# Two of four sums of weight quarters made by an adding DMA, and the second output block with its sign turned, in the gate and up products of a streaming encoder

## The chip, the cores and the metric

The kernel runs on one core of one Trainium2 chip. The metric is the device time of one execution of the whole kernel in microseconds (us); lower is better.

## The reference

One step of a two-layer encoder with 512 prompt rows and 64 sample rows of width 1024 (T = 576 rows in all), in float32. A layer has three parallel mixers, a cross-attention over 256 memory rows, and a gated feed-forward block. The change is in the last of these:

```
h = rmsnorm(x, g_ffn_norm)
x = x + (silu(h @ w_gate) * (h @ w_up)) @ w_down
```

`w_gate` and `w_up` are 1024 x 2816, `w_down` is 2816 x 1024.

## The kernel before

**Products.** Every float32 matmul is done in three: each operand is split into a high half H (rounded, made by ScalarE's copy, `copyA`) and a low half L (the rest, made by VectorE as source minus H; `split_to`, L467). `mm3` (L443) then adds H.H, H.L and L.H in PSUM. A weight tile is the stationary operand, 128 x 128; the activations, transposed, stream by with half of the 576 rows, HF = 288 columns.

**The feed-forward block.** The 2816 hidden columns are 11 pairs p of 256. Pair 0 (`first`) is computed plainly while the normalised activations of the second half become ready. For pairs 1 to 10, `gated` (L1696) computes two 1024 x 256 by 1024 x 576 products, gate and then up, each by a scheme of seven products instead of eight: the weight block and the activation block are each cut into 2 x 2 quarters, a11 (first 512 input rows, first 128 output columns), a12 (last 512 rows, first 128 columns), a21 (first 512 rows, last 128 columns), a22, and seven products of sums of quarters are combined. `wino_w` (L600) loads the 256 weight columns into a 1 MB tile (`wraw`, two buffers), makes the sums, and splits everything. `winograd` (L635) runs the products in the order 1, 2, 6, 5, 7, 4, 3, each 12 matmuls of 288 columns. It keeps intermediate results in PSUM or, through ScalarE, in tiles named `part`. VectorE adds the parts into gate and up tiles; `WNorm.sums` (L571) makes the matching sums of activation quarters once per layer.

**The weight side of the seven products, before.** Products 1, 2 and 4 use a11, a12 and a22. The other four use sums made by VectorE into two tiles named `sum`: s1 = a21 + a22 (product 5), s2 = s1 - a11 (product 6), z1 = a11 - a21 (product 7), z2 = a12 - s2 (product 3). Each tile of two sums is split together into tiles `sH` and `sL` (two buffers each): products 6 and 5 share one, products 7 and 3 the other. The plain quarters are split into `wH` and `wL` (three buffers each), which the down products use as well.

**Order of the work.** A pass of gate or up takes seven products; between up of one pair and gate of the next, half of the down product (`down`, L1751) of an earlier group of pairs runs. Each engine executes its own list of instructions, in an order that is fixed when the program is built from dependencies, buffer counts and estimated durations; the text's order gives priority, so weight splits for the next pass stand among the evacuations of the present one. A new load waits until the last reader of the buffer's old content is done. SyncE's queue issues the weight loads. GpSimd's queue is used at the kernel's start alone.

Of the kernel before, what the change touches and what calls it, by code (L numbers as in the profile page):

```python
# [10 lines left out]
F32 = mybir.dt.float32  # L11
F32R = mybir.dt.float32r
U32 = mybir.dt.uint32
AF = mybir.ActivationFunctionType
# [11 lines left out]
HF = T // 2  # L26
KD = D // 128
# [203 lines left out]
def tile_hybrid(ctx, tc, ins, outs):  # L231
    clock = tc.clock = Clock()
    nc = Engines(tc)
# [9 lines left out]

    uid = [0]
    phase = ["in"]
    UB = {"u": 3, "j": 4, "kp": 3, "sg": 3, "R": 1, "oS": 2, "gate": 3}
    WB = {"wH": 3, "wL": 3}
    PB = {"D": 3, "S": 2, "T": 3}

    def nm(s):  # L250
        uid[0] += 1
        return f"{phase[0]}.{s}_{uid[0]}"
# [8 lines left out]
    turn = {"pool": None, "close": None}  # L261
# [47 lines left out]
    def copyA(out, in_, scale=None):  # L309
        if scale is None:  # L310
            act(out, in_, AF.Copy)
        else:
            act(out, in_, AF.Identity, scale=scale)

    def tt(out, a, b, op, eng=None):
        (eng or nc.vector).tensor_tensor(out, a, b, op=op)

    def stt(out, a, s, b, op0, op1):
        nc.vector.scalar_tensor_tensor(out, a, s, b, op0=op0, op1=op1)
# [3 lines left out]
    def fetch_w(src, kt, n, src2=None):  # L323
        n1 = n
        if src2 is not None:
            n += src2.shape[1]
        raw = clock.tile(wp.tile([128, 2048], F32, tag="wraw", name=nm("wraw"), bufs=2), "wraw", 2)
        raw = raw[:, :kt * n].rearrange("p (k n) -> p k n", n=n)
        nc.sync.dma_start(raw[:, :, 0:n1], src.rearrange("(k p) n -> p k n", p=128))
        if src2 is not None:  # L330
            nc.sync.dma_start(raw[:, :, n1:n], src2.rearrange("(k p) n -> p k n", p=128))
        return raw
# [134 lines left out]
    def split_to(src, H, L):  # L467
        copyA(H, src)
        tt(L, src, H, SUB)

    def rstd_bcast(acc, ones, r, scale=1.0):
        n = acc.shape[1]
        w = HF if n > 512 else n
        for c in range(0, n, w):
            d = ps_("T")[:, 0:w]
            mm(d, ones, acc[:, c:c + w])
            act(r[:, c:c + w], d, AF.Ln, scale=scale, bias=eps1)
        act(r, r, AF.Exp, scale=-0.5)
# [49 lines left out]
    class WNorm:  # L528
# [42 lines left out]
        def sums(self):  # L571

            n = 4 * HF
            b11, b21, b12, b22 = (self.x[i][:, q * n:(q + 1) * n] for i in range(2) for q in range(2))
            t = big(name="tA")
            x, y = t[:, 0:n], t[:, n:2 * n]
            Ha, La, Hb, Lb = (big(F32R, "bT") for _ in range(4))
            tt(x, b12, b11, SUB)
            tt(y, b22, x, SUB)
            split_to(y, Ha[:, n:2 * n], La[:, n:2 * n])  # L580
            split_to(x, Ha[:, 0:n], La[:, 0:n])
            tt(x, b22, b12, SUB)
            split_to(x, Hb[:, 0:n], Lb[:, 0:n])
            tt(y, b21, y, SUB)
            split_to(y, Hb[:, n:2 * n], Lb[:, n:2 * n])
            self.p.update({5: (Ha, La, 0), 6: (Ha, La, 1), 7: (Hb, Lb, 0), 4: (Hb, Lb, 1)})

# [11 lines left out]

    def wino_w(src):  # L600

        raw = fetch_w(src, KD, 256)
        a11, a12, a21, a22 = (raw[:, q * 4:q * 4 + 4, m * 128:(m + 1) * 128] for m in range(2) for q in range(2))

        def split(x, own):
            H, L = (clock.tile((turn["pool"] if own else wp).tile([128, 1024], F32R, tag=tag, name=nm(tag),
                                                                  bufs=2 if own else WB[tag]), tag, 2 if own else WB[tag])
                    for tag in (("sH", "sL") if own else ("wH", "wL")))
            n = x.shape[1] * 128
            H, L = (y[:, 0:n].rearrange("p (k n) -> p k n", n=128) for y in (H, L))  # L610
            split_to(x, H, L)
            return H, L

        def sums():
            return clock.tile(turn["pool"].tile([128, 1024], F32, tag="sum", name=nm("sum"), bufs=2), "sum",
                              2).rearrange("p (k n) -> p k n", n=128)

        out = {}
        A = split(raw[:, :, 0:128], False)
        out[1], out[2] = (A, 0), (A, 4)  # L620
        s = sums()
        s2, s1 = s[:, 0:4, :], s[:, 4:8, :]
        tt(s1, a21, a22, ADD)
        tt(s2, s1, a11, SUB)
        B = split(s, True)
        out[6], out[5] = (B, 0), (B, 4)
        z = sums()
        tt(z[:, 0:4, :], a11, a21, SUB)
        tt(z[:, 4:8, :], a12, s2, SUB)
        C = split(z, True)  # L630
        out[7], out[3] = (C, 0), (C, 4)
        out[4] = (split(a22, False), 0)
        return out

    def winograd(w, xf, put):  # L635


        def product(d, p, more=False):

            (H, L), k0 = w[p]  # L640
            for k in range(4):
                mm3(d, H[:, k0 + k, :], L[:, k0 + k, :], xf.part(p, 0, k), xf.part(p, 1, k), not more and k == 0, k == 3, more)

        def keep(d):
            c = clock.tile(turn["pool"].tile([128, HF], F32, tag="part", name=nm("part"), bufs=4), "part", 4)
            copyA(c, d)
            return c

        x = ps_("D")[:, 0:HF]
        product(x, 1)  # L650
        c1 = keep(x)
        d = ps_("T")[:, 0:HF]
        product(d, 2)
        put(0, 0, d, c1)
        yield
        product(x, 6, True)
        c2 = keep(x)
        y = ps_("S")[:, 0:HF]
        product(y, 5)
        product(x, 7, True)  # L660
        c3 = keep(x)
        put(1, 1, y, c3)
        d = ps_("T")[:, 0:HF]
        product(d, 4)
        put(1, 0, d, c3)
        product(y, 3, True)
        put(0, 1, y, c2)
# [268 lines left out]
    def layer(l, xn):  # L936
# [759 lines left out]
        def gated(p, aH, aL, k0):  # L1696

            cs = lambda a: slice(a * HF, (a + 1) * HF)
            done, done2 = [0, 0], [0, 0]
            s = [u("gate") for _ in range(2)]  # L1700

            def gate(m, a, d, c):
                tt(s[m][:, cs(a)], d, c, ADD)
                done[m] += 1
                if done[m] == 2:
                    act(s[m], s[m], AF.Silu)

            run(winograd(wino_w(I["w_gate"][l, :, p * 256:(p + 1) * 256]), xf, gate))
            t = [u() for _ in range(2)]

            def up_(m, a, d, c):
                tt(t[m][:, cs(a)], d, c, ADD)
                done2[m] += 1
                if done2[m] == 2:
                    tt(t[m], t[m], s[m], MUL)
                    split_to(t[m], aH[:, k0 + m, :], aL[:, k0 + m, :])

            run(winograd(wino_w(I["w_up"][l, :, p * 256:(p + 1) * 256]), xf, up_))

# [117 lines left out]
```

## Time and profile before

| what | value |
|---|---|
| median of 3 runs | 1663.23 us (1661.26 to 1664.08) |
| the profiled execution | 1666.25 us |
| its span | 1664.5 us |
| TensorE (PE) busy | 1638.2 us (98%) |
| TensorE weight load (PEld) busy | 1532.3 us (92%) |
| VectorE (DVE) busy | 1216.0 us (73%) |
| ScalarE (ACT) busy | 897.1 us (54%) |
| GpSimd (POOL) busy | 142.2 us (9%) |
| DMA, share of 16 engines on SyncE's queue | 25.0% |
| granted TensorE clock | 0.994 |

The span is the time from the first to the last instruction that the profiler saw; the execution is a little longer. Busy time of TensorE counts overlapping pipelined matmuls once. Every operation that goes through the kernel's recording helper has the line L209, so rows are told apart by their tiles: `ffn0.sum` is a tile named `sum` of layer 0's feed-forward block.

### The profile page before, as it was taken

What the parts mean: (1) busy time and instruction counts of PE and PEld (TensorE: products, weight loads), DVE (VectorE), ACT (ScalarE), POOL (GpSimd) and SP (SyncE); (2) the same over time, 40 slices, a digit from 0 to 9 for tenths busy, and PEclk for the clock granted to TensorE, in tenths of its full rate; (3) what the DMA queues carried; (4) which work ended last, traced back from release to release, by engine and by line L of the source; (5) the groups of instructions that cost most, each with busy time, mean ns of one, the idle gap of its engine ahead of it and who ended that gap; (6) DMA issues with size and microseconds to landing.
All of it is one profiled execution on the core that took longest, in us unless ns stands there. A gap on an engine that the chain in (4) does not pass through costs nothing.

```text
span 1664.5 us, 30858 instructions
## 1 busy us (share of the span) xinstructions
PE 1638.2 (98%) x12279; PEld 1532.3 (92%) x12279; DVE 1216.0 (73%) x2508; ACT 897.1 (54%) x1915; POOL 142.2 (9%) x257
## 2 busy tenths in 40 slices
PE   8999999999999999999999999999999999999998
PEld 7989788699999999999998889877999999999998
DVE  5747798876798767666667488987678877667663
ACT  6436778665754443344443457886667453344431
POOL 3112351000000000000010133300000000000000
PEclk9999999999999999999999999999999999999999
DMA  5322230022123232322223313201211232332321
GB/s 168 118 69 65 75 111 26 27 77 77 52 77 102 77 102 77 102 93 85 81 75 97 93 40 118 67 27 39 89 52 56 97 102 77 102 99 79 101 77 58
DMA packets 113647, 133.30 MB, mean 80 GB/s; under 512 B 10610, under 2 KB 95712, under 8 KB 113504
## 3 DMA queue, kind: packets, MB, share of 16 engines
q1 hardware_dynamic: 113120, 131.30, 25.0%
q8 instruction: 97, 1.59, 0.4%
q14 instruction: 46, 0.38, 0.1%
q0 software_dynamic: 352, 0.03, 0.0%
q10 hardware_dynamic: 32, 0.01, 0.0%
HBM read 123.64 MB, written 7.68 MB: 79 GB/s over the span
## 4 chain that ended last, share of the span: by engine, by line
PE 81%; DVE 7%; issue 4%; ACT 3%; DMA 2%; POOL 1%; ACTq 0%; POOLq 0%; DVEq 0%
PE ffn0.D L209 10%; PE ffn1.D L209 9%; PE ffn0.T L209 7%; PE ffn0.S L209 7%; PE ffn1.T L209 6%; PE ffn1.S L209 6%; PE win1.D L209 6%; PE win0.D L209 4%; PE wout1.D L209 3%; PE wout0.D L209 3%; PE cross1.D L209 2%; PE cross0.D L209 2%; PE cross0.T L209 1%; PE cross1.T L209 1%; PE mlap0.T L209 1%
## 5 line engine op out<-in xcount | busy, mean ns | idle before, releaser
L209 ACT ACTIVATE ffn1.wH<-ffn1.wraw 128x1024 fp32r<-128x1024 f32 x64 | 59.4, 927 | 116.9 <-PE ffn1.T L209 61.7
L209 ACT ACTIVATE ffn0.wH<-ffn0.wraw 128x1024 fp32r<-128x1024 f32 x64 | 59.3, 927 | 111.5 <-PE ffn0.T L209 60.4
L209 DVE TENSOR_TENSOR ffn1.sL<-ffn1.sum,ffn1.sH 128x1024 fp32r<-128x1024 f32 x40 | 48.9, 1222 | 40.0 <-ACT ffn1.sH L209 39.9
L209 DVE TENSOR_TENSOR ffn0.sL<-ffn0.sum,ffn0.sH 128x1024 fp32r<-128x1024 f32 x40 | 48.9, 1222 | 39.6 <-ACT ffn0.sH L209 39.5
L209 DVE TENSOR_TENSOR ffn1.wL<-ffn1.wraw,ffn1.wH 128x1024 fp32r<-128x1024 f32 x64 | 67.6, 1056 | 8.3 <-ACT ffn1.wH L209 7.6
L209 DVE TENSOR_TENSOR ffn0.wL<-ffn0.wraw,ffn0.wH 128x1024 fp32r<-128x1024 f32 x64 | 67.5, 1055 | 8.3 <-ACT ffn0.wH L209 7.6
L209 PE MATMUL ffn0.D<-ffn0.bT,ffn0.sH 128*128 128x288 f32 x320 | 65.3, 296 | 0.1
L209 PE MATMUL ffn1.D<-ffn1.bT,ffn1.sH 128*128 128x288 f32 x320 | 65.1, 295 | 0.1
L209 ACT ACTIVATE ffn1.sH<-ffn1.sum 128x1024 fp32r<-128x1024 f32 x40 | 42.2, 1055 | 21.4 <-PE ffn1.S L209 21.2
L209 ACT ACTIVATE ffn0.sH<-ffn0.sum 128x1024 fp32r<-128x1024 f32 x40 | 42.2, 1055 | 21.1 <-PE ffn0.S L209 21.0
L209 POOL TENSOR_TENSOR win1.s<-win1.vg,rS 128x32 f32<-128x32 f32 (+1 forms) x5 | 2.9, 590 | 581.3 <-DVE win1.vg L209 580.2
L209 PEld LDWEIGHTS ffn0.D<-ffn0.bT,ffn0.sH 128*128 128x128 f32 x320 | 51.6, 189 | 1.0 <-ACT ffn0.part L209 0.6
L209 PEld LDWEIGHTS ffn1.D<-ffn1.bT,ffn1.sH 128*128 128x128 f32 x320 | 51.6, 189 | 0.7 <-ACT ffn1.part L209 0.6
L209 PE MATMUL ffn1.D<-ffn1.bT,ffn1.sL 128*128 128x288 f32 x160 | 47.5, 297 | 0.0
L209 PE MATMUL ffn0.D<-ffn0.bT,ffn0.sL 128*128 128x288 f32 x160 | 47.5, 297 | 0.0
L209 PE MATMUL win1.D<-win1.wH,ffn0.hH 128*128 128x256 f32 (+1 forms) x160 | 47.2, 295 | 0.0
L209 PE MATMUL win0.D<-win0.wH,in.hH 128*128 128x256 f32 (+1 forms) x160 | 47.1, 295 | 0.0
L209 PE MATMUL win0.D<-win0.wL,in.hH 128*128 128x256 f32 (+1 forms) x160 | 46.1, 288 | 0.3 <-DVE win0.wL L209 0.3
L209 PE MATMUL win1.D<-win1.wL,ffn0.hH 128*128 128x256 f32 (+1 forms) x160 | 46.1, 288 | 0.3 <-DVE win1.wL L209 0.3
L209 PE MATMUL win0.D<-win0.wH,in.hL 128*128 128x256 f32 (+1 forms) x160 | 45.9, 287 | 0.0
L209 PE MATMUL win1.D<-win1.wH,ffn0.hL 128*128 128x256 f32 (+1 forms) x160 | 45.9, 287 | 0.0
L209 ACT ACTIVATE ffn0.part<-ffn0.D 128x288 f32<-128x288 f32 x60 | 24.5, 409 | 38.4 <-PE ffn0.D L209 38.4
(972 smaller groups left out, 6522.2 us busy)
## 6 DMA issues: line engine op xcount, KB each, us to landing
ffn0.wraw<-in_w_gate_dram SPq DMA_DIRECT2D x11, 1024.0 KB, 5.3
ffn0.wraw<-in_w_up_dram SPq DMA_DIRECT2D x11, 1024.0 KB, 5.3
ffn0.wraw<-in_w_down_dram SPq DMA_DIRECT2D x11, 1024.0 KB, 5.1
ffn1.wraw<-in_w_gate_dram SPq DMA_DIRECT2D x11, 1024.0 KB, 5.3
ffn1.wraw<-in_w_up_dram SPq DMA_DIRECT2D x11, 1024.0 KB, 5.4
ffn1.wraw<-in_w_down_dram SPq DMA_DIRECT2D x11, 1024.0 KB, 5.0
win1.wraw<-in_w_in_dram SPq DMA_DIRECT2D x7, 1024.0 KB, 5.4
win0.wraw<-in_w_in_dram SPq DMA_DIRECT2D x6, 1024.0 KB, 5.7
```

Source lines behind the costliest of these rows:

```text
L209: r = fn(*args, **kw)
```

## The change

The second output block of gate and up (the last 128 columns of each pair) is computed with its sign turned. With a21 and a22 replaced by their negatives, all sums become plain additions: s1 = a21 + a22 (product 5), s3 = a11 + a21 (product 7), s2 = s1 + a11 (product 6), s4 = s2 + a12 (product 3), up to signs that move to the activation sums and to the output: `WNorm.sums` forms its sums with other signs and splits one of them with `split_neg`, the Silu of the second block gets a scale of -1, and the split of the second block's product is done by `split_neg`.

s1 and s3 are no longer made by VectorE. SyncE's queue loads a11 into the raw tile, a12 and a22 into the raw tile, a22 a second time into a new tile `sumD` (s1's place) and a11 a second time (s3's place). Then GpSimd's queue loads a21 twice, adding to s1 and to s3. VectorE adds s2 and s4 into a tile `sum`. Products 6 and 3 now share one split (F), products 5 and 7 the other (E). `sumD` has two buffers, `sum` one instead of two, the gate tiles two instead of three, `part` three instead of four.

```diff
-    UB = {"u": 3, "j": 4, "kp": 3, "sg": 3, "R": 1, "oS": 2, "gate": 3}
+    UB = {"u": 3, "j": 4, "kp": 3, "sg": 3, "R": 1, "oS": 2, "gate": 2}
...
+    def split_neg(src, H, L):
+        copyA(H, src, scale=-1.0)
+        stt(L, src, -1.0, H, MUL, SUB)
...
-            tt(x, b12, b11, SUB)
-            tt(y, b22, x, SUB)
-            split_to(y, Ha[:, n:2 * n], La[:, n:2 * n])
+            tt(x, b11, b12, SUB)
+            tt(y, b22, x, ADD)
+            split_neg(y, Ha[:, n:2 * n], La[:, n:2 * n])
...
-            tt(y, b21, y, SUB)
+            tt(y, y, b21, SUB)
...
-        raw = fetch_w(src, KD, 256)
-        a11, a12, a21, a22 = (raw[:, q * 4:q * 4 + 4, m * 128:(m + 1) * 128] for m in range(2) for q in range(2))
+        raw = clock.tile(wp.tile([128, 2048], F32, tag="wraw", name=nm("wraw"), bufs=2), "wraw", 2).rearrange("p (k n) -> p k n", n=256)
+        e, f = (clock.tile(turn["pool"].tile([128, 1024], F32, tag=tag, name=nm(tag), bufs=n), tag, n)
+                .rearrange("p (k n) -> p k n", n=128) for tag, n in (("sumD", 2), ("sum", 1)))
+        rows = src.rearrange("(k p) n -> p k n", p=128)
+        a11, a12, a21, a22 = ((slice(q * 4, q * 4 + 4), slice(m * 128, (m + 1) * 128)) for m in range(2) for q in range(2))
+        nc.sync.dma_start(raw[:, 0:4, 0:128], rows[:, a11[0], a11[1]])
+        nc.sync.dma_start(raw[:, 4:8, :], rows[:, 4:8, :])
+        s1, s3, s2, s4 = e[:, 0:4, :], e[:, 4:8, :], f[:, 0:4, :], f[:, 4:8, :]
+        for x, y in ((s1, a22), (s3, a11)):
+            nc.sync.dma_start(x, rows[:, y[0], y[1]])
+        for x in (s1, s3):
+            nc.pool_queue.dma_start(x, rows[:, a21[0], a21[1]], accum_op=ADD)
...
-        s = sums()
-        s2, s1 = s[:, 0:4, :], s[:, 4:8, :]
-        tt(s1, a21, a22, ADD)
-        tt(s2, s1, a11, SUB)
-        B = split(s, True)
-        out[6], out[5] = (B, 0), (B, 4)
-        z = sums()
-        tt(z[:, 0:4, :], a11, a21, SUB)
-        tt(z[:, 4:8, :], a12, s2, SUB)
-        C = split(z, True)
-        out[7], out[3] = (C, 0), (C, 4)
-        out[4] = (split(a22, False), 0)
+        tt(s2, s1, raw[:, 0:4, 0:128], ADD)
+        tt(s4, s2, raw[:, 4:8, 0:128], ADD)
+        F = split(f, True)
+        out[6], out[3] = (F, 0), (F, 4)
+        E = split(e, True)
+        out[5], out[7] = (E, 0), (E, 4)
+        out[4] = (split(raw[:, 4:8, 128:256], False), 0)
...
-            c = clock.tile(turn["pool"].tile([128, HF], F32, tag="part", name=nm("part"), bufs=4), "part", 4)
+            c = clock.tile(turn["pool"].tile([128, HF], F32, tag="part", name=nm("part"), bufs=3), "part", 3)
...
-                    act(s[m], s[m], AF.Silu)
+                    act(s[m], s[m], AF.Silu, scale=-1.0 if m else 1.0)
...
-                    split_to(t[m], aH[:, k0 + m, :], aL[:, k0 + m, :])
+                    (split_neg if m else split_to)(t[m], aH[:, k0 + m, :], aL[:, k0 + m, :])
```

## Rows read from the trace of the kernel before

**Rows 1.** The page: busy us (share of the span) and instructions of each engine.
```profile
PE 1638.2 (98%) x12279; PEld 1532.3 (92%) x12279; DVE 1216.0 (73%) x2508; ACT 897.1 (54%) x1915; POOL 142.2 (9%) x257
```
**Rows 2.** Stretches: from:to, length, busy us and instructions, clock, DMA share, GB/s.
```profile
435.00:440.00 5.00, 5.00 (x40) 5.00 (x39) 5.00 (x11) 3.67 (x7) 0.00 (x0) 1.00 0.59 198
...
455.00:460.00 5.00, 5.00 (x40) 5.00 (x40) 4.85 (x5) 3.81 (x5) 0.00 (x0) 1.00 0.00 0
...
440.00:476.00 36.00, 34.29 (x250) 33.28 (x249) 32.72 (x43) 24.66 (x40) 0.00 (x0) 1.00 0.09 30
476.00:836.80 360.80, 360.68 (x2715) 359.80 (x2714) 260.63 (x404) 155.64 (x213) 0.00 (x0) 1.00 0.29 91
```
**Rows 3.** TensorE in order of time: start, us, instruction, [idle before, releaser].
```profile
445.65 0.40 PE L209 MATMUL ffn0.D<-cross0.bH,ffn0.wH 128*128 128x288 f32 x1 [0.65 <-ACT cross0.bH L209]
...
447.04 0.40 PE L209 MATMUL ffn0.D<-cross0.bL,ffn0.wH 128*128 128x288 f32 x1 [0.73 <-DVE cross0.bL L209]
```
**Rows 4.** Chain of waits, layer 0's feed-forward block: start, us, what.
```profile
504.85 1.59 PE ffn0.D L209 x12
...
579.64 1.86 PE ffn0.D L209 x12
...
611.72 1.59 PE ffn0.D L209 x12
...
614.91 1.76 PE ffn0.D L209 x12
616.67 1.59 PE ffn0.S L209 x12
...
638.93 1.59 PE ffn0.D L209 x12
```
**Rows 5.** The tile `ffn0.sum`: duration ns min/median/max, first and last start.
```profile
L209 DVE TENSOR_TENSOR ffn0.sum<-ffn0.wraw x40: 680/687/695, 434.4 to 769.3; 128x512 f32<-128x512 f32 x40
```
**Rows 6.** VectorE in order of time, columns as in rows 3.
```profile
437.64 0.69 DVE L209 TENSOR_TENSOR ffn0.sum<-ffn0.wraw,ffn0.sum 128x512 f32<-128x512 f32 x1
...
443.04 2.63 DVE L209 TENSOR_TENSOR cross0.xs<-cross0.xs,cross0.u 128x1152 f32<-128x1152 f32 x2
...
610.58 0.69 DVE L209 TENSOR_TENSOR ffn0.sum<-ffn0.wraw 128x512 f32<-128x512 f32 x1 [1.04 <-DMA ffn0.wraw<-in_w_gate_dram]
...
613.29 0.45 DVE L209 TENSOR_TENSOR ffn0.gate<-ffn0.S,ffn0.part 128x288 f32<-128x288 f32 x1
613.66 1.22 DVE L209 TENSOR_TENSOR ffn0.sL<-ffn0.sum,ffn0.sH 128x1024 fp32r<-128x1024 f32 x1
```
**Rows 7.** ScalarE in order of time, the same passage.
```profile
612.27 1.04 ACT L209 ACTIVATE ffn0.sH<-ffn0.sum 128x1024 fp32r<-128x1024 f32 x1
...
614.37 0.39 ACT L209 ACTIVATE ffn0.part<-ffn0.D 128x288 f32<-128x288 f32 x1
```
**Rows 8.** DMA issues: out<-in, queue, count, KB each, us to landing.
```profile
ffn0.wraw<-in_w_gate_dram SPq DMA_DIRECT2D x11, 1024.0 KB, 5.3
...
win0.pl<-in_cache_mla_latent_dram SPq DMA_DIRECT2D x1, 256.0 KB, 3.9
...
in.grow<-in_g_cqn_dram POOLq DMA_DIRECT2D x1, 1.0 KB, 4.8
...
in.grow<-in_g_qn_dram POOLq DMA_DIRECT2D x1, 0.5 KB, 6.3
```
**Rows 9.** SyncE's queue in order of time: start, us, issue.
```profile
428.91 0.37 SPq L209 DMA_DIRECT2D ffn0.wraw<-in_w_gate_dram  x1
...
480.58 0.37 SPq L209 DMA_DIRECT2D ffn0.wraw<-in_w_gate_dram  x1
...
605.12 0.37 SPq L209 DMA_DIRECT2D ffn0.wraw<-in_w_gate_dram  x1
```
**Rows 10.** GpSimd in order of time, an issue of a small load.
```profile
2.76 0.49 POOL L209 DMA_DIRECT2D in.grow<-in_g_mem_norm_dram  x1
```
**Rows 11.** Groups by line and form: busy us, mean ns; the two forms of subtraction.
```profile
L209 DVE TENSOR_TENSOR ffn0.actL<-ffn0.u,ffn0.actH 128x576 fp32r<-128x576 f32 x22 | 16.6, 752 | 0.1
...
L209 DVE SCALAR_TENSOR_TENSOR ffn0.hL<-X,gT,ffn0.hH 128x576 fp32r<-128x576 f32 x8 | 6.5, 816 | 0.9 <-ACT ffn0.hH L209 0.8
```

More of the change, by code (lines that the diff above doesn't have):

```diff
@@ L612, in split @@
             return H, L
-        def sums():
-            return clock.tile(turn["pool"].tile([128, 1024], F32, tag="sum", name=nm("sum"), bufs=2), "sum",
-                              2).rearrange("p (k n) -> p k n", n=128)
         out = {}
```

## The prediction
> **What bounds the kernel now.** I read the busy times first, then stretches of the run, then what TensorE waited for, then the two transfers and engines that the change touches. TensorE is busy 1638.2 of 1664.5 us [rows 1]. The stretch table says where the rest is [rows 2]: from 476.0 to 836.8 us, where the first layer's feed-forward block runs on the seven-product scheme, TensorE is busy 360.68 of 360.80 us, VectorE 260.63 and ScalarE 155.64. The reader should see that VectorE has 100 us to spare there. All 20 gate and up passes of a layer lie in this stretch, bar the first 3 us, and layer 1 repeats it. A product of 12 matmuls takes 1.59 us, one after another, in the chain of waits [rows 4]; six pieces of the layer are longer (1.86, 1.76, 1.72, 1.68, 1.74 and 1.86 us; the first and the second stand there), 1.08 us in all. The one place in which TensorE visibly waits near the change is the entry of the feed-forward block, 440 to 476 us, with 34.29 of 36 us busy: 0.65 us for the high half and 0.73 us for the low half of the scaled activations [rows 2, 3].
>
> **What the change does, part by part.**
>
> *Two additions of four leave VectorE.* One takes 0.687 us [rows 5]; per call of wino_w two go, 40 calls, so 80 x 0.687 = 55 us of VectorE work. In the steady stretch TensorE is the bound and VectorE idle 100 us per layer, so nothing of it reaches the end, except through the six late pieces: at 614.91 product 6 waits for the copy of product 1, which ScalarE started at 614.37 [rows 7] behind a Silu whose input VectorE delivered with the evacuation at 613.29 [rows 6]. An emptier VectorE can take between nothing and all of it: 0 to 1.1 us per layer. I take half a microsecond over both.
>
> *The entry.* VectorE is full from 435 to 440 [rows 2]; one addition at 437.64 stands ahead of the residual additions on which the scaling at 443.04 rests [rows 6]. If what leaves is really out of the way, TensorE's 0.65 + 0.73 us, all that is idle there but 0.3 us (36.00 - 34.29 = 1.7), may shrink: 0 to 1.7 us per layer. Against that, the two additions that stay now wait for a later transfer (rival C). I take a quarter of a microsecond per layer, 0.5 us.
>
> *The transfer gets longer.* Now: one load of 1024 KB lands after 5.3 us [rows 8]; it is issued at 605.12 [rows 9] and first used by an addition at 610.58, which had waited 1.04 us for it [rows 6]. The first product that needs a sum of this load is product 6 of the next gate pass, at 638.93 [rows 4]. After the change: four loads on SyncE's queue, 1280 KB in all. Nearest rows: 256 KB in rows of 512 bytes takes 3.9 us, 1024 KB 5.3 us [rows 8], so 768 KB more cost 1.4 us, and 1280 KB 5.8 us at least; one after the other, each paid in full, 3 x 3.9 + 5.3 = 17.0 us at most. I take 6.5 us, because the four queue behind each other without waiting for a landing. Then GpSimd waits for s1's load and issues the adding transfer. No row shows a transfer that adds. Below: a plain load of that size, 3.9 us. Above: the small GpSimd transfers of 0.5 to 1 KB took 4.8 to 6.3 us [rows 8], and adding could cost the 0.5 us per 256 KB (1.4 x 256 / 768) several times over; with four times that on the slowest, 6.3 + 2.0 = 8.3 us each, and the second one waiting for the first. I take 5.3, between the two rows, and 2 x 0.5 for reading two sides: 6.3 us. s1 is whole 12.8 us after the load's issue, s3 1.0 us later (one GpSimd issue, 0.49 us [rows 10], and one more transfer). The bounds are 5.8 + 3.9 = 9.7 us and 17.0 + 2 x 8.3 = 33.6 us.
>
> The Trainium skill, page "DMA: Bandwidth & Descriptors", section "Anatomy of one DMA — SWDGE (gpsimd) path", gives a GpSimd transfer 2.0 us plus its bytes at 436 GB/s. That would make 256 KB land 2.6 us after issue, as an estimate from that page, and s1 whole after 9.1 us; the rows of 4.8 to 6.3 us for a few hundred bytes are longer than that, so they go into my sum, and with the page's figure the forecast would be the same and rival B less likely.
>
> *Is the longer transfer covered?* For the load of 605.12: s1 at 617.9, two additions 1.37 us, the high half 1.04 us [rows 7], the low half 1.22 us [rows 6], so F is ready at 621.5, 17 us ahead of 638.93. The shortest cover is the second gate pass: issued at 480.58, ready at 497.0, needed at 504.85 [rows 4, 9]; 7.8 us. The worst bound, 33.6 + 3.6 = 37.2 us against 33.8 us of cover, would miss by 3.4 us per pass. At my value nothing shows. GpSimd has no instruction in these stretches [rows 2], so the 80 new issues there, about 40 to 60 us of its time, stand before nobody. On SyncE's queue three more issues per call stand ahead of the next load, 0.37 us each [rows 9]; each 1 MB of weights becomes 1.25 MB loaded and 0.5 MB added, against a DMA share of 0.29 now. TensorE doesn't feel transfers: 40 matmuls start in 435 to 440 us with a DMA share of 0.59, and 40 in 455 to 460 with none [rows 2].
>
> *Slots.* The raw tile is kept until its last split, that of a22, for which a weight buffer comes free only when TensorE is done with an earlier one; the additions, some 20 us ahead of their need, end before that, so it frees no later. Sums 6 and 3 now share one split, 5 and 7 the other. Product order is 1, 2, 6, 5, 7, 4, 3. Before, one slot came free after product 5 and the other at the end of the pass; the latter's successor was due at product 7. Now they come free after product 7 and at the end. With the slot freed first going to F, F has from 608.54 (611.72 less two products) to 614.91, and E from 611.72 to 616.67 [rows 4]; the chain in it is 1.04 + 1.22 us and handover, which today runs from 612.27 to 614.88 [rows 6, 7]. About 1.8 us stays, instead of 3.4 (product 7 starts at 616.67 + 1.59 = 618.26). With the slots the other way round F would have 3.2 us and still just fit. The part ring at 3 and the gate ring at 2 free on VectorE in the order in which it writes them: nothing.
>
> *Turned sign.* 10 low halves per layer go from a plain subtraction, 752 ns, to the scalar form, 816 ns [rows 11], 0.6 us of VectorE per layer, and one of 1152 columns with them, 0.1 us by the same ratio; all off the path. ScalarE's scale is an operand of the same pass.
>
> **The sum.** -0.5 (late pieces) - 0.5 (entry) + 0 (transfers, slots, sign) = -1.0 us. The profiled execution took 1666.25 us, so 1665.2; it lay 3.0 above the median of the runs, 1663.23, and the same 1.0 us off that gives **1662.2 us**.
>
> **The rivals.**
>
> *B, slower: VectorE stands at the addition.* An engine takes its instructions in a fixed order. If the addition keeps the place it has now, at 610.58, and s1 comes at 617.9, VectorE stands 7 us; behind it are the evacuation of product 3 and the low half that starts at 613.66 [rows 6], which product 5 of the up pass needs at 616.67. They would end at 617.9 + 0.69 + 0.45 + 1.22 = 620.3, TensorE 3.6 us late; nine gate-to-up passages per layer have the next load in flight, 18 x 3.6 = 65 us: 1728 us. It decides from the point at which the wait outlasts 614.3 (616.67 - 1.22 - 0.45 - 0.69). For it: today VectorE already stands 1.04 us at this very place, so it was put there as if the load landed earlier. Against it: the order is made anew with the added transfers in it, and an addition put 3 to 5 us later meets work with many microseconds to spare. A weak form, 1 us per passage, gives 1680.
>
> *C, slower: the same wait at the entry.* Load at 428.91 [rows 9], s1 at 441.7; an addition that stays at 437.64 would hold the residual additions and the scaling 4.1 us, less the 1.4 us of two removed additions: 2.7 us x 2 layers, 1668 us. For it, the full VectorE there; against it, that it may be ordered behind the scaling.
>
> *D, faster: the entry gains all it can.* 1.7 us and the late pieces' 1.1 us in both layers: 5.6 us, 1657.6. For it, the additions stand before the critical ones; against it, that the scaling also needs ScalarE's squares and TensorE's sum, so the shift is not passed on whole.
>
> *E: adding is far slower than copying,* near the bound of 33.6 us: 3.4 us x 38 passes, 1792 us. Nothing in the rows speaks for it; nothing excludes it.
>
> **How the numbers follow.** Forecast 0.55 (its own range 1660 to 1665), B 0.15, C 0.15, D 0.12, E 0.03. What the measurement can tell from no change is about 0.2%, 3.3 us. Faster: most of D and a little of the forecast's spread, 0.12. Slower: B, E, most of C and a little of the spread, 0.32. Same: 0.56. The range 1658.5 to 1684 leaves out half of D below and E and the strong half of B above.
>
> **What would show it.** In the changed profile, steady stretches with TensorE busy as fully as now; VectorE some 55 us less busy in all, GpSimd at work through the feed-forward blocks; additions of s1 that start 10 to 15 us after the first load's issue; TensorE's waits at the entry still near 0.7 us each. I am wrong if TensorE waits for an sL, a T or an S bank in the steady stretch and VectorE waits for the adding transfer just before (B), or if the scaling at the entry starts later than now (C).

## The result, and the profile after

The changed kernel took 1680.37 us (median of 4 runs, 1678.37 to 1682.29), the kernel before beside it 1663.32: a ratio of 1.0104, interval 1.0086 to 1.0122, 17 us slower. The profiled execution took 1682.04 us with a span of 1680.3.

The page's busy times after, against [rows 1]:

```profile
PE 1645.3 (98%) x12279; PEld 1533.6 (91%) x12279; DVE 1165.9 (69%) x2428; ACT 892.1 (53%) x1915; POOL 244.9 (15%) x337
```

VectorE lost 50 us of work, where 55 were forecast; GpSimd gained 103, where 40 to 60 were forecast. TensorE does the same 12279 matmuls and is 7 us busier. The stretches that answer to [rows 2] (from:to, length, then busy us and instructions of PE, PEld, DVE, ACT, POOL, then granted clock, DMA share, GB/s):

```profile
439.00:475.00 36.00, 35.26 (x259) 34.39 (x258) 32.68 (x42) 24.91 (x42) 0.00 (x0) 1.00 0.00 1
475.00:843.10 368.10, 365.18 (x2713) 361.69 (x2712) 236.84 (x367) 153.23 (x213) 46.68 (x36) 1.00 0.56 131
486.00:489.20 3.20, 0.37 (x3) 0.13 (x1) 1.69 (x4) 1.05 (x4) 0.00 (x0) 0.93 0.75 123
489.20:492.20 3.00, 2.91 (x12) 2.91 (x13) 2.70 (x4) 0.98 (x2) 0.00 (x0) 0.50 0.10 27
1312.10:1315.80 3.70, 0.33 (x3) 0.09 (x2) 2.29 (x5) 1.68 (x4) 0.00 (x0) 0.87 0.60 100
1315.80:1321.40 5.60, 5.60 (x23) 5.60 (x24) 2.41 (x3) 1.23 (x2) 1.18 (x2) 0.50 0.56 159
```

Layer 0's entry is a little better (35.26 of 36 us busy instead of 34.29), but its steady stretch is 368.1 us long instead of 360.7. In each layer there is one place, 486 and 1312 us, where TensorE does nearly nothing for 3 us and more, and behind it a time at a granted clock of 0.50: 1.2 GHz, with 12 matmuls in 3.0 us and 23 in 5.6, where a run below (e12) does 25 in the same 3.0 us at a clock of 1.00. Three costs can be told apart.

**The first gate-to-up passage of a layer.** This is where the last product of a gate pass (product 3) is followed by the up pass of the same pair. TensorE, ScalarE, VectorE, GpSimd and SyncE's queue (SPq) there, each in order of time (start, us, instruction, [idle before, and what ended it]), and then VectorE at the same place in the kernel before:

```profile
489.29 0.85 PE L209 MATMUL ffn0.D<-ffn0.bT,ffn0.sH 128*128 128x288 f32 x2 [2.92 <-ACT ffn0.part L209]
...
483.52 1.06 ACT L209 ACTIVATE ffn0.wH<-ffn0.wraw 128x1024 fp32r<-128x1024 f32 x1 [2.40 <-DMA ffn0.wraw<-in_w_down_dram]
...
488.26 0.68 ACT L209 ACTIVATE ffn0.gate<-ffn0.gate 128x576 f32<-128x576 f32 x1 [2.15 <-DVE ffn0.gate L209]
488.85 0.39 ACT L209 ACTIVATE ffn0.part<-ffn0.D 128x288 f32<-128x288 f32 x1
...
487.16 0.69 DVE L209 TENSOR_TENSOR ffn0.sum<-ffn0.sumD,ffn0.wraw 128x512 f32<-128x512 f32 x1 [1.32 <-DMA ffn0.sumD<-in_w_gate_dram]
487.77 0.45 DVE L209 TENSOR_TENSOR ffn0.gate<-ffn0.S,ffn0.part 128x288 f32<-128x288 f32 x1
...
477.90 2.58 POOL L209 DMA_DIRECT2D ffn0.sumD<-in_w_gate_dram  x2 [62.42 <-DVE ffn0.sum L209]
...
474.19 0.92 SPq L209 DMA_DIRECT2D ffn0.sumD<-in_w_gate_dram  x2
475.46 0.37 SPq L209 DMA_DIRECT2D ffn0.wraw<-in_w_down_dram  x1
```
```profile
484.71 0.45 DVE L209 TENSOR_TENSOR ffn0.gate<-ffn0.S,ffn0.part 128x288 f32<-128x288 f32 x1
...
486.36 1.29 DVE L209 TENSOR_TENSOR ffn0.sum<-ffn0.wraw 128x512 f32<-128x512 f32 x2
```

Read it backwards. TensorE waits for the copy of product 1, that stands behind a Silu, the Silu waits for VectorE's evacuation at 487.77 (the addition that empties product 3's PSUM bank into the gate tile), and this stands behind an addition that waits until 487.16 for the adding transfer of the second pair's gate weights. VectorE stood idle for 1.32 us and could have done the evacuation then; its order had the addition first, where the kernel before had the evacuation (484.71) ahead of the additions of the same pass (486.36).

The load that s1 starts from was issued at 474.19, and s1 came whole 13.0 us later, where 12.8 was forecast. That the two agree is luck: SyncE's queue had the two loads of `sumD` first and those of the raw tile only at 478.81, so GpSimd issued 3.7 us after the load instead of 6.5, and the adding transfer took 9.2 us instead of 6.3. The load of the down projection, on the queue behind the loads of `sumD`, is late as well and holds the high half at 483.52.

**The steady pairs.** The chain of waits, ScalarE and VectorE beside it, and ScalarE at the end of a product 7 in the kernel before:

```profile
614.74 1.20 PE ffn0.D L209 x9
615.93 1.77 PE ffn0.S L209 x12
617.71 0.40 PE ffn0.D L209 x3
```
```profile
613.10 1.06 ACT L209 ACTIVATE ffn0.sH<-ffn0.sum 128x1024 fp32r<-128x1024 f32 x1 [2.68 <-PE ffn0.D L209]
614.07 0.39 ACT L209 ACTIVATE ffn0.part<-ffn0.D 128x288 f32<-128x288 f32 x1
...
614.19 1.23 DVE L209 TENSOR_TENSOR ffn0.sL<-ffn0.sum,ffn0.sH 128x1024 fp32r<-128x1024 f32 x1 [4.49 <-ACT ffn0.sH L209]
615.34 0.45 DVE L209 TENSOR_TENSOR ffn0.gate<-ffn0.S,ffn0.part 128x288 f32<-128x288 f32 x1
```
```profile
606.85 1.06 ACT L209 ACTIVATE ffn0.sH<-ffn0.sum 128x1024 fp32r<-128x1024 f32 x1 [1.04 <-PE ffn0.S L209]
608.57 0.41 ACT L209 ACTIVATE ffn0.part<-ffn0.D 128x288 f32<-128x288 f32 x1 [0.66 <-PE ffn0.D L209]
```

Product 3 (on the S bank) takes 1.77 us instead of 1.59. The end of product 7 at 613.1 makes two things possible at once: the copy of that product (`part`), and, because 5 and 7 now share a slot that comes free here, the next pass's split (`sH`, `sL`). The split runs first on both engines. So the copy comes at 614.07 and the evacuation of the S bank at 615.34, and product 3, which adds to that bank, waits for it. In the kernel before the end of product 5 released the split, one product earlier, and ScalarE was free when the copy came due at 608.57. TensorE's order already has 9 matmuls of the next product ahead of product 3, and still three pieces of each pair are 0.13 to 0.18 us too long (product 3 of gate, product 6 and product 3 of up); the kernel before had six such pieces in the whole layer, all of them product 6 of up, two of them in [rows 4].

**Layer 1's entry.** VectorE there, after and then before; and the time from issue to landing (all data there) of an adding transfer and a plain load of that passage, and of the same plain load at layer 0's entry (out<-in, queue, count, KB each, us to landing):

```profile
1257.34 0.69 DVE L209 TENSOR_TENSOR ffn1.sum<-ffn1.sumD,ffn1.wraw 128x512 f32<-128x512 f32 x1 [2.90 <-DMA ffn1.wraw<-in_w_gate_dram]
1257.94 1.22 DVE L209 TENSOR_TENSOR ffn1.wL<-ffn1.wraw,ffn1.wH 128x1024 fp32r<-128x1024 f32 x1
```
```profile
1251.03 1.23 DVE L209 TENSOR_TENSOR ffn1.wL<-ffn1.wraw,ffn1.wH 128x1024 fp32r<-128x1024 f32 x1
...
1253.25 0.69 DVE L209 TENSOR_TENSOR ffn1.sum<-ffn1.wraw 128x512 f32<-128x512 f32 x1 [0.26 <-DMA ffn1.wraw<-in_w_gate_dram]
```
```profile
ffn1.sumD<-in_w_up_dram POOLq DMA_DIRECT2D x2, 256.0 KB, 8.7
...
ffn1.wraw<-in_w_gate_dram SPq DMA_DIRECT2D x1, 256.0 KB, 5.7
...
ffn0.wraw<-in_w_gate_dram SPq DMA_DIRECT2D x1, 256.0 KB, 2.9
```

The addition waits not for an adding transfer but for the plain load of a11. That load took 5.7 us beside four adding transfers; in layer 0, where those had been made long before, 2.9. But the load is only a part of it: in the kernel before the addition there rested on the whole 1024 KB, which landed after 5.3 us, and VectorE waited 0.26 us. What differs is the place. There a split's low half (1.23 us) and two operations of 0.45 us stood ahead of the addition; in the changed kernel they stand behind it, so of the 2.90 us some 2 are the place and some 0.5 the later landing.

### The profile page after: what moved, and what is told of

Read it like the earlier page. It is cut to its first block, busy times and chain, and to the rows that moved or that the text cites. A ratio compares the mean times of both kernels' runs of the same rounds, so it can differ in the third digit from the quotient of the medians.

```text
span 1680.3 us, 31229 instructions
## 1 busy us (share of the span) xinstructions
PE 1645.3 (98%) x12279; PEld 1533.6 (91%) x12279; DVE 1165.9 (69%) x2428; ACT 892.1 (53%) x1915; POOL 244.9 (15%) x337
## 3 DMA queue, kind: packets, MB, share of 16 engines
q0 software_dynamic: 42592, 21.01, 10.2%
q8 instruction: 97, 1.59, 0.4%
## 4 chain that ended last, share of the span: by engine, by line
PE 82%; DVE 8%; ACT 3%; issue 3%; DMA 2%; POOL 1%; ACTq 0%; POOLq 0%; DVEq 0%; SPq 0%
PE ffn0.D L209 9%; PE ffn1.D L209 9%; PE ffn0.S L209 7%; PE ffn1.S L209 7%; PE ffn0.T L209 6%; PE ffn1.T L209 6%; PE win1.D L209 6%; PE win0.D L209 4%; PE wout1.D L209 3%; PE cross0.D L209 3%; PE wout0.D L209 3%; PE cross1.D L209 2%; PE cross1.T L209 1%; PE cross0.T L209 1%; PE mlap1.T L209 1%
## 5 line engine op out<-in xcount | busy, mean ns | idle before, releaser
L209 DVE TENSOR_TENSOR ffn1.sL<-ffn1.sum,ffn1.sH 128x1024 fp32r<-128x1024 f32 x20 | 24.5, 1225 | 76.6 <-ACT ffn1.sH L209 76.6
L209 DVE TENSOR_TENSOR ffn0.sL<-ffn0.sum,ffn0.sH 128x1024 fp32r<-128x1024 f32 x20 | 24.5, 1225 | 75.1 <-ACT ffn0.sH L209 75.1
L209 POOL DMA_DIRECT2D ffn1.sumD<-in_w_gate_dram x20 | 25.9, 1508 | 292.5 <-DVE cross1.ocL L209 141.7
L209 POOL DMA_DIRECT2D ffn0.sumD<-in_w_gate_dram x20 | 26.0, 1512 | 288.3 <-DVE X L209 173.2
L209 ACT ACTIVATE ffn1.sH<-ffn1.sum 128x1024 fp32r<-128x1024 f32 x20 | 21.2, 1061 | 51.1 <-PE ffn1.D L209 51.1
L209 POOL DMA_DIRECT2D ffn0.sumD<-in_w_up_dram x20 | 27.0, 1649 | 144.7 <-DMA ffn0.sumD<-in_w_up_dram 125.1
L209 ACT ACTIVATE ffn0.sH<-ffn0.sum 128x1024 fp32r<-128x1024 f32 x20 | 21.2, 1061 | 49.8 <-PE ffn0.D L209 49.8
L209 POOL DMA_DIRECT2D ffn1.sumD<-in_w_up_dram x20 | 26.2, 1584 | 145.4 <-DMA ffn1.sumD<-in_w_up_dram 145.4
```

Source lines behind the costliest of these rows:

```text
L209: r = fn(*args, **kw)
```

## The experiments

All are kernels of their own, timed beside the kernel before. The table gives the ratio to it with its interval, and three lengths from one profiled execution of each, from the start of the first matmul of one stage to that of the next: the steady stretch of layer 0 (first product on the activation sums `bT` to `win1.D`) and of layer 1 (to `out.D`), and layer 1's entry (first matmul of `cross1` to the first on `cross1.bH`).

| kernel | ratio | layer 0 | layer 1 | entry 1 |
|---|---|---|---|---|
| before | | 360.66 | 356.09 | 90.57 |
| changed | 1.0104 (1.0086 to 1.0122) | 368.22 | 365.79 | 93.14 |
| e1 | 1.0055 (1.0043 to 1.0068) | 364.32 | 360.08 | 90.67 |
| e2 | 1.0337 (1.0319 to 1.0355) | 388.34 | 384.17 | 90.49 |
| e3 | 1.0000 (0.9991 to 1.0009) | 360.65 | 356.09 | 90.68 |
| e4 | 1.0051 (1.0037 to 1.0064) | 363.95 | 359.71 | 90.58 |
| e5 | 1.0082 (1.0069 to 1.0095) | 367.34 | 362.75 | 91.25 |
| e6 | 1.0736 (1.0721 to 1.0751) | 417.31 | 417.17 | 93.24 |
| e7 | 1.0655 (1.0642 to 1.0669) | 416.92 | 410.02 | 90.52 |
| e8 | 1.0053 (1.0039 to 1.0067) | 364.87 | 361.84 | 90.44 |
| e9 | 0.9998 (0.9989 to 1.0007) | 359.84 | 355.57 | 90.73 |
| e10 | 0.9990 (0.9981 to 0.9999) | 359.42 | 355.18 | 90.60 |
| e11 | 1.0017 (1.0008 to 1.0026) | 360.50 | 356.37 | 92.94 |
| e12 | 1.0048 (1.0035 to 1.0060) | 364.38 | 360.45 | 95.27 |
| e13 | 0.9987 (0.9977 to 0.9997) | 359.42 | 355.16 | 90.55 |
| e14 | 0.9988 (0.9980 to 0.9997) | 359.42 | 355.16 | 90.65 |

**e3: the sign and the rings alone.** The kernel before with the second block's sign turned, gate at 2 buffers and part at 3; the old pairs.

> The kernel before with only the turned sign and the shorter rings (gate 2, part 3): old pairing, VectorE sums. Both theories: 1663 us within 0.2%. If the sign's scalar form or the shorter rings cost, up to 1670 us, with TensorE waiting for a part or gate buffer.

1662.08 us, the two stretches the same to 0.01 us, layer 1's entry to 0.11. Sign and rings cost nothing.

**e1: the new pairs, sums by VectorE.**

```diff
-        for x in (s1, s3):
-            nc.pool_queue.dma_start(x, rows[:, a21[0], a21[1]], accum_op=ADD)
...
+        tt(s1, raw[:, 0:4, 128:256], raw[:, 4:8, 128:256], ADD)
+        tt(s3, raw[:, 0:4, 128:256], raw[:, 0:4, 0:128], ADD)
```

> The changed kernel's pairing of the sums (6 with 3, 5 with 7), its turned sign and its rings, but all four sums made by VectorE from one 1024 KB load; no transfer adds. Theory (two causes): of the 17.1 us, the wait for the adding transfer at the first gate-to-up passage of each layer with the half clock behind it (about 4.6 us in layer 0 and 6.3 in layer 1) and the wait at layer 1's entry (2.6) go; the steady product waits stay, three per pair of some 0.15 to 0.2 us, 3.0 to 3.2 us per layer. Time 1669 us, feed-forward stretch about 364 us per layer. Rival 1 (the adding transfer is the cause of all of it): 1663 us, no steady waits. Rival 2 (the pairing is the cause of all): 1678 to 1681 us, the 3 us gap at the first passage still there.

1672.10 us, 3 us above the theory. No gap at the first passage, no cost at layer 1's entry, and product 3 as late as in the changed kernel. About half of the loss is there without any adding transfer: 9 of 17 us by the times, 3.7 and 4.0 us by the lengths of the two layers, where the theory had 3.0 to 3.2 each.

**e4 and e12: fewer adding transfers.** In e4 three passes of a layer go back to one load and VectorE's sums; in e12 only the second pair's gate pass.

```diff
+        if byV:
+            nc.sync.dma_start(raw, rows)
...
-            run(winograd(wino_w(I["w_gate"][l, :, p * 256:(p + 1) * 256]), xf, gate))
+            run(winograd(wino_w(I["w_gate"][l, :, p * 256:(p + 1) * 256], p == 2), xf, gate))
```

> The changed kernel, but the first three gate and up passes on the seven-product scheme (gate and up of the first pair, gate of the second) take their four sums on VectorE from one load; the other 17 passes of a layer keep the adding transfers. Theory (two causes): the 3 us gap at the first passage, the half clock behind it and the wait at layer 1's entry go (13 us), the steady waits stay (6.2 us): 1667 to 1669 us. Rival 1 (adding transfer costs in every pass): 1678 us, since 34 of 40 passes keep it. Rival 2 (pairing is all): 1680 us.

> The changed kernel with one pass per layer altered: the gate pass of the second pair takes its sums on VectorE from one load. Theory: the 3.2 and 3.7 us at the first passage are VectorE's stand at this pass's sum, which waits for its adding transfer; they and the half clock behind them go (4 us in layer 0, 6 in layer 1), the steady waits and layer 1's entry stay: 1670 to 1672 us. Rival (the stall is the late load of the down projection's weights, or the adding transfers of the first pair): 1678 to 1681 us.

1670.05 and 1670.38 us. In e12 one pass of 20 is altered, and at the first passage, where [rows 2]'s counterpart above had 0.37 us busy of 3.20, the same stretch reads

```profile
486.00:489.20 3.20, 3.20 (x26) 3.20 (x26) 2.17 (x3) 0.41 (x1) 0.24 (x1) 1.00 0.64 184
489.20:492.20 3.00, 3.00 (x25) 3.00 (x24) 1.33 (x2) 2.24 (x3) 2.31 (x2) 1.00 1.07 280
```

So this one pass's adding transfers, with the half clock behind the wait, cost 3.8 us in layer 0 and 5.3 in layer 1 (the changed kernel's lengths less those of e12). The time of e12 is as its theory had it; e4 lies 1 us above its own. The rival, the late down load, is not parted from the wait by e12: there that load lands after 4.8 us, in the changed kernel after 8.0. e11 below parts them. e12's entry of layer 1 came out 2.1 us longer than the changed kernel's: there VectorE stood 4.34 us for the same plain load, TensorE 2.89, and the clock fell to 0.53 behind it. This is one execution, at 1673.37 us the longest of the five.

**e5: copy instead of add.**

```diff
-            nc.pool_queue.dma_start(x, rows[:, a21[0], a21[1]], accum_op=ADD)
+            nc.pool_queue.dma_start(x, rows[:, a21[0], a21[1]])
```

> The changed kernel with the two GpSimd transfers of each pass copying instead of adding (the sums s1 and s3 then hold only the quarter a21: the two added terms are left out); same bytes read, same queue, same waits. Theory A (adding itself is dear): the transfers land after 4 to 5 us instead of 7.1 and 5.9, GpSimd's issue falls below 1.5 us, the 3.2 and 3.7 us gaps at the first passage shrink to about 1 us without half clock behind them: 1673 to 1675 us. Theory B (GpSimd's queue and the place behind the load are dear, adding is not): landing 6 to 7 us, gaps as they are, 1679 to 1681 us.

The two sums lack the terms a22 and a11 that were to be added to. 1675.55 us, between the theories. The page's lines on these transfers, of the changed kernel and then of e5 (queue: packets, MB, share of 16 engines; then landings; then GpSimd's issues with count, busy us and mean ns):

```profile
q0 software_dynamic: 42592, 21.01, 10.2%
...
L209 POOL DMA_DIRECT2D ffn0.sumD<-in_w_gate_dram x20 | 26.0, 1512 | 288.3 <-DVE X L209 173.2
...
ffn0.wraw<-in_w_down_dram SPq DMA_DIRECT2D x11, 1024.0 KB, 7.6
...
ffn0.sumD<-in_w_gate_dram POOLq DMA_DIRECT2D x20, 256.0 KB, 7.1
ffn0.sumD<-in_w_up_dram POOLq DMA_DIRECT2D x20, 256.0 KB, 5.9
```
```profile
q0 software_dynamic: 6752, 21.01, 4.1%
...
L209 POOL DMA_DIRECT2D ffn0.sumD<-in_w_gate_dram x20 | 15.1, 756 | 299.3 <-DVE X L209 178.5
...
ffn0.sumD<-in_w_gate_dram POOLq DMA_DIRECT2D x20, 256.0 KB, 6.1
ffn0.sumD<-in_w_up_dram POOLq DMA_DIRECT2D x20, 256.0 KB, 4.6
```

Adding costs 1.0 to 1.3 us of landing, twice GpSimd's time per issue and six times the packets. Most of the landing time is there without adding. The gaps at the first passage shrank only to 2.10 and 3.25 us between matmul starts, from 3.22 and 3.67. Theory A had 1 us, because it left out that a second transfer is late there: VectorE now waits 0.57 and 1.70 us at the same addition for the plain load of a11 into the raw tile, which is issued behind the loads of `sumD` and of the down projection and in layer 0 lands after 7.1 us.

**e2, e6, e8, e7: other slots.** e2 has the old pairs with adding transfers; e6 to e8 give each sum its own slot (four of half the size), with adding transfers (e6), with VectorE's sums (e8), and with the first three passes by VectorE (e7).

```diff
...
-        F = split(f, True)
-        out[6], out[3] = (F, 0), (F, 4)
-        E = split(e, True)
-        out[5], out[7] = (E, 0), (E, 4)
+        for q, x in ((6, s2), (3, s4), (5, s1), (7, s3)):
+            out[q] = (split(x, True), 0)
```

> The changed kernel with the pairing of the kernel before (6 with 5, 7 with 3), two sums still made by adding transfers, three sum buffers of 4 KB as in the change. Theory (two causes): the steady product waits go (6.2 us over both layers), the first passage with its half clock and layer 1's entry stay: 1673 to 1675 us. Rival 1 (adding transfer is all): 1680 us. Rival 2 (pairing is all): 1663 us.

> The changed kernel with each of the four sums split into a slot of its own (512 columns, 4 slots of half the size, the same memory; each comes free with its own product), so that no split waits for a partner's product; adding transfers in every pass stay. Theory (the steady waits are the pair slot that comes free at the end of product 7): the waits at product 3 and its neighbours go, 3.4 to 3.9 us per layer, the first passage with the half clock and layer 1's entry stay: 1672 to 1674 us. Rival (the steady waits come from the order of the additions or from the part ring of 3): they stay, 1680 us.

> Single slots and all four sums on VectorE from one load (the first run of the study with the slots parted). Theory: the product waits of that run, 3.8 and 4.0 us per layer, go: 1661 to 1664 us. Rival (they come from pairing sum 6 with sum 3 in time, not from the slots): 1672 us again.

> Single slots, and the first three passes of a layer sum on VectorE, the other 17 by adding transfers. Theory (two causes and nothing else): both are gone, 1661 to 1664 us, no change against the kernel before, although VectorE does some 45 us less. Rival (an adding transfer costs something in every pass, or an emptier VectorE gains): 1668 us and over, or 1658 and under.

1718.24, 1784.62, 1671.00 and 1770.61 us: all four miss their theory. e8, which comes out as its rival had it, took away the partner's wait and not the loss. Its ScalarE rows say why: at the end of product 7 a split, now half as long, still runs ahead of the copy.

```profile
608.08 0.63 ACT L209 ACTIVATE ffn0.sH<-ffn0.sumD 128x512 fp32r<-128x512 f32 x1 [1.01 <-PE ffn0.D L209]
608.62 0.39 ACT L209 ACTIVATE ffn0.part<-ffn0.D 128x288 f32<-128x288 f32 x1
```

e6 and e7 show rival B's strong form. In e7, VectorE in a steady pair, and the transfers that it waits for:

```profile
606.53 0.69 DVE L209 TENSOR_TENSOR ffn0.sum<-ffn0.sumD,ffn0.wraw 128x512 f32<-128x512 f32 x1 [5.07 <-DMA ffn0.sumD<-in_w_up_dram]
...
607.75 0.45 DVE L209 TENSOR_TENSOR ffn0.u<-ffn0.S,ffn0.part 128x288 f32<-128x288 f32 x1
...
599.28 2.57 POOL L209 DMA_DIRECT2D ffn0.sumD<-in_w_up_dram  x2 [23.14 <-DVE ffn0.wL L209]
...
595.56 0.92 SPq L209 DMA_DIRECT2D ffn0.sumD<-in_w_up_dram  x2
```

The tile of s1 and s3 comes free only with the later of two splits, at 595.5. Load, adding transfer and addition follow, 11.0 us, and VectorE stands 5.07 of them ahead of the evacuation that product 3 needs. With such waits the stretch of a layer is 54 to 61 us longer in e6 and e7. In e2, with three tiles for the sums of two passes, TensorE stands 0.6 to 5.4 us between two matmul starts nine times in layer 0 and eleven times in layer 1; what it was made for, the old pairs without another change, it doesn't tell.

**e9, e11, e10: the splits in order.** The splits of a pass are put behind the copy of product 7 of the pass before on ScalarE, and behind its evacuation on VectorE: e1, the changed kernel and e4 with no other edit. (`last` holds the latest instruction of each engine, and `behind` orders its first argument after the second.)

```diff
             split_to(x, H, L)
+            if own and seven:
+                for e in ("act", "dve"):
+                    behind(tc, last[e], seven[e])
...
         c3 = keep(x)
+        seven["act"] = last["act"]
         put(1, 1, y, c3)
+        seven["dve"] = last["dve"]
```

> The new pairing with all sums on VectorE (run e1), and the splits of a pass ordered behind the copy of product 7 of the pass before on ScalarE, and behind the evacuation that uses it on VectorE; nothing else. Parting the slots did not take the steady waits away (run e8), and its timeline shows a split that the end of product 7 releases running ahead of that copy, so that product 3 finds its bank 0.2 us late. Theory (two small operations are overtaken by the split): the waits at product 3 go, 1662 to 1665 us. Rival (the waits come from the pairing in another way, such as the later split itself): 1670 to 1672 us.

> The changed kernel with nothing but the order of the splits: adding transfers in all passes. Theory: the steady waits go (3.4 to 3.9 us per layer), the first passage with the half clock behind it and layer 1's entry stay: 1672 to 1674 us. Rival: 1680 us, or 1690 and over if the wait for the adding transfer enters every pair.

> The same order of the splits, with the first three passes of a layer on VectorE and the other 17 by adding transfers (run e4 with the order). Theory: nothing of the change's cost is left, 1661 to 1665 us. Rival 1: 1670 us as in e4, if the order does not help. Rival 2 (as in the runs with single slots and adding transfers, a later freed sum slot brings the wait for the adding transfer into every pair): 1690 us and over.

1662.23, 1665.73 and 1660.98 us. e9's steady stretches are 4.5 us per layer shorter than e1's. The passage of e11 that answers to the steady one above:

```profile
608.45 0.41 ACT L209 ACTIVATE ffn0.part<-ffn0.D 128x288 f32<-128x288 f32 x1 [2.76 <-PE ffn0.D L209]
608.76 1.05 ACT L209 ACTIVATE ffn0.sH<-ffn0.sum 128x1024 fp32r<-128x1024 f32 x1
...
608.89 0.46 DVE L209 TENSOR_TENSOR ffn0.gate<-ffn0.S,ffn0.part 128x288 f32<-128x288 f32 x1 [3.92 <-ACT ffn0.part L209]
609.84 1.23 DVE L209 TENSOR_TENSOR ffn0.sL<-ffn0.sum,ffn0.sH 128x1024 fp32r<-128x1024 f32 x1 [0.49 <-ACT ffn0.sH L209]
```
```profile
610.00 1.59 PE ffn0.S L209 x12
```

The copy goes first, the bank is free at 609.35, and product 3 starts at 610.00 and takes 1.59 us. Which of the two orders, ScalarE's or VectorE's, would do alone was not tried. e11 did better than the theory: the first passage lost its half clock too. With the orders made anew, the evacuation there stands ahead of the addition (rows of e11's VectorE), and 0.80 us of TensorE's 2.92 are left. The down load is as late as in the changed kernel (7.7 us to landing, its high half at 483.49 instead of 483.52), so it can account for those 0.80 us at most: the rest of the wait is the addition's place. In layer 1, 0.93 of 3.37 us are left.

```profile
485.73 0.45 DVE L209 TENSOR_TENSOR ffn0.gate<-ffn0.S,ffn0.part 128x288 f32<-128x288 f32 x1
486.66 0.69 DVE L209 TENSOR_TENSOR ffn0.sum<-ffn0.sumD,ffn0.wraw 128x512 f32<-128x512 f32 x1 [0.48 <-DMA ffn0.wraw<-in_w_gate_dram]
```

**e13 and e14: what is left, and what gains.** e13 is the kernel before with this order and nothing of the change. e14 is e11 with the first gate pass of a layer by VectorE (p == 1 in e12's line).

> The kernel before, with nothing of the change, but the splits of a pass ordered behind the copy and the evacuation of product 7 of the pass before. Theory (the order of small operations and splits is what matters, the pairing and the transfers are not): the late pieces of the kernel before, 1.1 us per layer, shrink as in the two runs with the order, 1661 to 1663 us. Rival (the old pairing needs its first split early, since its slot comes free after product 5 and product 6 of the next pass is due sooner after a later split): TensorE waits for sH or sL, 1668 us and over.

> Splits in order and adding transfers in all passes but one per layer: the gate pass of the first pair sums on VectorE from one 1024 KB load. Theory (VectorE stands at layer 1's entry because the first addition rests on a 256 KB load that was put on the queue behind and beside the adding transfers and lands after 5.7 us, not 2.9): with the additions resting on the whole load they are placed later, layer 1's entry goes back to 90.6 us, 2.4 less, and the time to 1662 to 1663.5 us. Rival (the adding transfers of the first up pass, still there, make any load late): entry 92 to 93 us, 1665 us.

1659.92 and 1660.69 us, both 0.1% below the kernel before and 1 us below their theories. e14's gate load at layer 1's entry, one of 1024 KB, landed after 5.4 us with no adding transfer beside it; its first addition has the place that it has in the kernel before, behind the split's low half, VectorE waits 0.35 us, and the entry is back at 90.65 us. In e13 the steady stretch of layer 0 is full:

```profile
475.00:834.40 359.40, 359.40 (x2714) 359.40 (x2713) 259.27 (x404) 153.95 (x213) 0.00 (x0) 1.00 0.29 92
```

e13 and e14 have the same two lengths, 359.42 and 355.16. With the order right, the 44 us less on VectorE (1170.0 us busy in e14, 1213.8 in e13) are worth nothing, and the 0.1% comes from the order alone.

## Why the prediction was wrong

The forecast of no change fell. The time lay inside the range, whose upper part had been set for rivals B and C; some 8 of the 17 us came from a cause that no rival had. By its steps:

- *Slots* failed. The working asked whether F and E are split in time for their own products, found 1.8 us to spare, and stopped. That they are in time holds. What it left out is what a split runs ahead of: 1.06 and 1.23 us of split on two engines, released at the very moment at which a copy of 0.4 us and an evacuation of 0.45 us became due, for which product 3 has one product's time. e9 and e11 show it with an edit that moves only the splits. Size: 3.7 and 4.0 us per layer (e1), where the step had nothing.
- *Is the longer transfer covered?* failed in its question, not in its total. s1 whole after 13.0 us at the first passage and 11.0 in e7 stand against 12.8, by two terms that were off by 3 us each way at the first passage; adding itself costs 1.0 to 1.3 us against 1.0. But the cover was counted to the product that needs the sum, "7.8 us" for the second gate pass. What counts is VectorE's order: the addition stood ahead of an evacuation for which TensorE waited from 486.37 on, 22 us before the product 6 that needs the sum (508.50). This is rival B, given 0.15 and priced at nine passages per layer; it came at one per layer, with its 3 us and a half clock that no part of the prediction had: 3.8 and 5.3 us (e12).
- *The entry* had the right sign in layer 0 only: 90.68 us became 90.21. In layer 1 it is rival C's place and price, 2.6 us against 2.7, but by luck, since the cause is another. The addition waited for a plain load, not for an adding transfer, and it waited mostly because it had been put ahead of some 2 us of other work of VectorE (e14, with the old place, has no loss); the load itself landed 0.5 us later than the whole one did before.
- *Late pieces* were worth more than taken: up to 1.1 us per layer was the bound, and 1.2 and 0.9 go. But it is the order that takes them away (e13), not the emptier VectorE.
- *Turned sign* and the rings at nothing: right (e3).
- *GpSimd's issues*: 103 us instead of 40 to 60, 1.5 us each; they stand before nobody, as said.
- Rival E is out: e14 keeps 19 of 20 adding passes per layer and loses nothing.

By lengths the sum is 8.1 us for the order of the splits (e12 against before; e1 would say 7.7), 9.2 for the first passages (the changed kernel against e12), 2.6 for layer 1's entry and -0.5 for layer 0's: 19.4 us, where the runs have 17.1, interval 14.3 to 20.3. The profiled executions differ by up to 3.5 us in layer 1's attention, whose code is the same in all of them, so the last 2 us of such a sum say nothing.

What stays open: why the orders came out as they did was not tried. That the addition at layer 1's entry was put early because a load of a quarter's size was reckoned to land sooner fits e14, and is argued, not shown.

## What to carry to other kernels

When a buffer's release is moved, ask what the release lets loose and what else is due at that moment on the same engines; a long operation that is early may stand ahead of a short one that is due. When a sum or a load is made later, count its cover to the first instruction behind it in its engine's order, not to its own consumer. A change that only relieves an engine with spare time gains nothing; look for the place where the order of that engine is at fault, as here, where putting two small operations ahead of a split gave 0.1% and 44 us less work on VectorE gave nothing.

## What the runs showed of the hardware

- Behind a 2.92 us wait TensorE's granted clock was 0.50, 1.2 GHz, for 3.0 us, and behind 3.37 us for 5.6. It does not follow every such wait: in e5, of the 60 matmuls behind its gap of 2.10 us between starts 16 ran at half speed, of those behind its gap of 3.25 us (2.96 us idle) 2. With it, the two waits cost 3.8 and 5.3 us.
- A GpSimd transfer of 256 KB landed after 7.1 and 5.9 us when adding (packets of about 0.5 KB, 21.01 MB in 42592) and after 6.1 and 4.6 when copying (about 3.1 KB). By the fit in the Trainium skill, page "DMA: Bandwidth & Descriptors", section "Anatomy of one DMA — SWDGE (gpsimd) path", 2.0 us and the bytes at 436 GB/s, it would be 2.6 us as an estimate; the measurement decides.
- Plain loads pay for them: the 1024 KB load of the down projection landed after 7.6 us (median of 11) instead of 5.1, and after 5.3 in e11, which issues the same transfers at other times. With transfers that only copy (e5) it is 7.2.
